# Splitting a weight stream into high and low parts one half chunk further ahead of the matmuls

## The chip, the core and the metric

The kernel runs on one core of a Trainium2 chip. Its engines work side by side, each through its own queue in program order: TensorE (PE in the profile; its weight loads are PEld), VectorE (DVE), ScalarE (ACT), GpSimd (POOL) and SyncE (SP, which only issues DMA transfers here). Engines wait for each other by semaphores. The metric is the device time of one execution in microseconds (us), the median of three runs.

## What is computed

Two layers of a decoder block on 256 tokens of width 1024, all in float32: a half-step SwiGLU feed-forward (ffn1), a mixer that adds dilated attention and a gated linear recurrence, a cross-attention into 256 memory tokens, and a second feed-forward (ffn2).

```python
for l in range(DEPTH):                                   # DEPTH = 2
    x = x + 0.5 * swiglu(rms_norm(x, ffn1_norm[l]), ffn1_w_gu[l], ffn1_w_down[l])
    h = rms_norm(x, mix_norm[l])
    z = h @ w_in[l]                                      # 1024 -> 10752
    ...
    merged = sigmoid(gate_a) * y_a + sigmoid(gate_b) * y_b
    x = x + merged @ w_mix_out[l]
    x = x + cross_attention(rms_norm(x, xattn_norm[l]), rms_norm(mem, mem_norm[l]), ...)
    x = x + 0.5 * swiglu(rms_norm(x, ffn2_norm[l]), ffn2_w_gu[l], ffn2_w_down[l])
return rms_norm(x, final_norm)
```

## The kernel before

**Split weights.** Every product with a weight is made of fp32r matmuls on two parts: `whi`, the weight rounded to fp32r, and `wlo`, the weight minus `whi`. The activations are split in the same way and lie in a `slot` as high and low halves side by side. One weight block is 128x128. In the usual form (`fm`, L325 and L326, and `fm_beside`, L338 and L339) a block takes two matmuls: `whi` against 512 columns (both halves of the activation) and `wlo` against 256 columns.

**The stream.** Class `Stream` holds all weight blocks in the order of their use. A chunk is 16 blocks (1 MB, one DMA, tile `raw`, three buffers); a half chunk is 8 blocks, numbered here from 0 to 535 through the whole program. For each half chunk ACT writes `whi` from `raw` (L104, a cast of 128x1024) and DVE writes `wlo` from `raw` and `whi` (L110). The first four half chunks are made in pieces before the loop (`first`, L74 and L75). The load of chunk c+2 goes into the buffer of chunk c-1, so SP issues it when the last `wlo` of chunk c-1 is done.

**The order.** The program is written out in the order of execution (`manual_schedule`): each engine runs its instructions as the Python code emits them. The clock of that code is `take`, called for each group of blocks. At the first block of half chunk i it runs `on_half`, which is `tick`: the deferred work that has come due (adding a result's halves, L349; multiplying by the norm, L521; activation functions, L522; splitting the result into a `slot`, L279 on ACT and L282 on DVE) and one step of the side work (memory statistics, rope tables, lower bounds, recurrence, attention). Behind that, `prep` emits the casts up to half chunk i+3 and the low parts up to i+2. So what DVE has to do at step i stands in its queue ahead of the low part that PE wants at step i+2. Results are copied out of PSUM by ACT (`L346`) as soon as a `pair` is complete; in the residual form (`Resid.take`) DVE adds them to x (L438), ACT and DVE write the next layer's split operand (L289, L290) and the sum of squares (L376, L378).

**Stages that matter here.** In ffn1 of layer 1 the side work of the whole program (memory statistics, rope tables, lower bounds) runs beside the feed-forward. At the end of the mixer, eight pairs of 12 blocks (`w_att_branch`, `w_hgrn_branch`) are multiplied by the gates (L927, L929) and split; then `mm_resid` of `w_mix_out` runs four outputs side by side (`fm_beside`, 32 blocks), followed by two `fm` of two outputs each (16 blocks each).

**Buffers.** `his` has 5 tiles of 4 KB per partition, `los` 4, and `big`, the pool of the slots, 27.

Of the kernel before, what the change touches and what calls it, by code (L numbers as in the profile page):

```python
# [46 lines left out]
class Stream:  # L47
# [65 lines left out]
    def take(self, descs):  # L113

        n = len(self.order)
        i, o = divmod(n, HALF)
        assert o + len(descs) <= HALF
        self.order.extend(descs)
        if o == 0:
            if i == 0:  # L120
                self.prep(i + 3, i + 2)
            self.on_half()
            self.prep(i + 3, i + 2)
            self.hi.pop(i - 1, None)
            self.lo.pop(i - 1, None)
        s = slice(o * P, (o + len(descs)) * P)
        return self.hi[i][:, s], self.lo[i][:, s]


def build(tc, a, nchunks):  # L130
    nc = tc.nc
    ctx = ExitStack()
    ent = ctx.enter_context
    consts = ent(tc.tile_pool(name="consts", bufs=1))
    raws = ent(tc.tile_pool(name="raws", bufs=3))
    his = ent(tc.tile_pool(name="his", bufs=5))
    los = ent(tc.tile_pool(name="los", bufs=4))
    big = ent(tc.tile_pool(name="big", bufs=27))
    mid = ent(tc.tile_pool(name="mid", bufs=4))
    tmps = ent(tc.tile_pool(name="tmps", bufs=10))  # L140
    tiny = ent(tc.tile_pool(name="tiny", bufs=2))
# [981 lines left out]
```

## Time and profile before

| what | value |
|---|---|
| median of 3 runs | 1645.06 us (1644.39 to 1645.84) |
| profiled execution | 1648.55 us, of which the span from the first to the last instruction is 1646.8 us |
| PE busy | 1624.9 us, 99% of the span |
| PE weight loads busy | 1415.4 us, 86% |
| DVE busy | 1242.6 us, 75% |
| ACT busy | 924.7 us, 56% |
| granted TensorE clock, mean over the span | 0.997 |
| DMA | 288.92 MB, mean 175 GB/s |

The profile is of one execution. The ends of matmuls are modelled and they overlap, so the 99% of PE is not a statement that nothing can be gained; the waits and the distances from start to start tell more. A share of busy time is a mean over stages that differ.

### The profile page before, as it was taken

The page shows a single profiled execution, that of the slowest core. Times are in us where ns is not written, and L with a number is a line of the kernel's source. Part 1 is how long each engine was busy: PE and PEld are TensorE (multiplying, and loading weights), DVE is VectorE, ACT ScalarE, POOL GpSimd, SP SyncE. Part 2 cuts the span into 40 slices and gives each one's busy share as a digit, 9 for nine tenths or more (in the row PEclk, how much of TensorE's full clock was granted, in tenths as well). Part 3 has the DMA queues.
Part 4 walks back from the last instruction along what each step waited for, and adds up shares of the span by engine and source line. Part 5 has one row for each costly group of instructions (what it writes and reads, how often), then busy time and mean ns, then how long its engine had stood idle before and what let it go on. Part 6 is the DMA issues. An engine that isn't in the chain of part 4 may idle for free.

```text
span 1646.8 us, 26215 instructions
## 1 busy us (share of the span) xinstructions
PE 1624.9 (99%) x10818; PEld 1415.4 (86%) x10818; DVE 1242.6 (75%) x1804; ACT 924.7 (56%) x1381; POOL 64.6 (4%) x46
## 2 busy tenths in 40 slices
PE   9999999999999999999999999999999999999998
PEld 7888888888887888888888888888888878888887
DVE  7888577777878777777677776777688787688764
ACT  6666454556555556565455655546565555566642
POOL 0000000102200000000000000001111000000000
PEclk9999999999999999999999999999999999999999
DMA  7555554443445444555445554544344444455552
GB/s 283 185 185 215 183 187 169 155 160 126 176 152 181 179 154 156 199 183 205 179 179 186 198 213 172 193 169 152 132 152 163 169 178 157 152 186 198 181 200 80
DMA packets 41591, 288.92 MB, mean 175 GB/s; under 512 B 4864, under 2 KB 4992, under 8 KB 7424
## 3 DMA queue, kind: packets, MB, share of 16 engines
q1 hardware_dynamic: 41040, 286.67, 48.0%
q8 instruction: 85, 1.39, 0.3%
q10 hardware_dynamic: 432, 0.59, 0.1%
q14 instruction: 34, 0.28, 0.0%
HBM read 286.18 MB, written 1.05 MB: 174 GB/s over the span
## 4 chain that ended last, share of the span: by engine, by line
PE 90%; DVE 5%; ACT 4%; issue 1%; DMA 0%; POOLq 0%; ACTq 0%; DVEq 0%
PE pair L325 48%; PE pair L326 25%; PE pair L299 3%; PE pair L300 3%; PE pair L301 3%; ACT whi L104 2%; PE bank L656 1%; DVE wlo L110 1%; DVE join L349 1%; PE pair L338 1%; DVE join L927 1%; PE pair L754 1%; PE bank L787 1%; ACT join L346 1%; PE pair L339 1%
## 5 line engine op out<-in xcount | busy, mean ns | idle before, releaser
L325 PE MATMUL pair<-slot,whi 128*128 128x512 f32 x3744 | 1321.5, 397 | 0.0
L326 PE MATMUL pair<-slot,wlo 128*128 128x256 f32 x3744 | 1049.1, 280 | 7.2 <-DVE wlo L110 7.2
L325 PEld LDWEIGHTS pair<-slot,whi 128*128 128x128 f32 x3744 | 703.6, 188 | 162.2 <-DVE slot L282 0.4
L326 PEld LDWEIGHTS pair<-slot,wlo 128*128 128x128 f32 x3744 | 707.9, 189 | 10.9 <-DVE wlo L110 9.8
L110 DVE TENSOR_TENSOR wlo<-raw,whi 128x1024 fp32r<-128x1024 f32 x532 | 641.1, 1224 | 27.9 <-ACT whi L104 27.1
L104 ACT CAST whi<-raw 128x1024 fp32r<-128x1024 f32 x532 | 540.0, 1045 | 13.7 <-issue 5.6
L349 DVE TENSOR_TENSOR join<-pair,join 128x512 f32<-128x512 f32 x136 | 93.9, 691 | 122.1 <-ACT join L346 121.8
L346 ACT COPY join<-pair 128x512 f32<-128x512 f32 x136 | 79.3, 584 | 98.4 <-PE pair L326 98.3
L289 ACT ACTIVATE slot<-x,vecs 128x256 fp32r<-128x256 f32 x64 | 30.8, 505 | 138.6 <-DVE x L438 137.2
L522 ACT ACTIVATE tmp<-join 128x256 f32<-128x256 f32 x88 | 36.5, 418 | 117.9 <-DVE join L521 117.8
L279 ACT CAST slot<-join 128x256 fp32r<-128x256 f32 (+1 forms) x120 | 51.8, 435 | 69.3 <-DVE join L929 31.1
L299 PE MATMUL pair<-whi,slot 128*128 128x512 f32 x224 | 88.9, 397 | 0.0
L300 PE MATMUL pair<-wlo,slot 128*128 128x512 f32 x224 | 87.6, 391 | 0.7 <-DVE wlo L110 0.7
L301 PE MATMUL pair<-whi,slot 128*128 128x512 f32 x224 | 87.4, 390 | 0.0
L438 DVE SCALAR_TENSOR_TENSOR x<-pair,x 128x256 f32<-128x256 f32 (+1 forms) x80 | 42.4, 530 | 54.4 <-PE pair L326 49.6
L346 ACT COPY slot<-pair 128x512 f32<-128x512 f32 x48 | 28.1, 585 | 78.9 <-PE pair L326 78.9
L349 DVE TENSOR_TENSOR slot<-pair,slot 128x512 f32<-128x512 f32 x48 | 33.1, 689 | 40.7 <-ACT slot L346 40.7
L521 DVE TENSOR_TENSOR join<-join,bc 128x512 f32<-128x512 f32 x88 | 60.5, 692 | 3.9 <-ACT bc L414 1.2
L890 POOL TENSOR_TENSOR join<-join,sinb 128x512 f32<-128x512 f32 x24 | 43.7, 1820 | 414.1 <-ACT join L889 402.8
L282 DVE TENSOR_TENSOR slot<-join,slot 128x256 fp32r<-128x256 f32 (+1 forms) x120 | 53.4, 454 | 2.8 <-ACT slot L279 2.8
L300 PEld LDWEIGHTS pair<-wlo,slot 128*128 128x128 f32 x224 | 42.1, 188 | 9.6 <-DVE wlo L110 1.6
L290 DVE SCALAR_TENSOR_TENSOR slot<-x,vecs,slot 128x256 fp32r<-128x256 f32 x64 | 29.6, 484 | 27.2 <-ACT slot L289 27.2
(192 smaller groups left out, 1088.7 us busy)
## 6 DMA issues: line engine op xcount, KB each, us to landing
raw<-w SPq DMA_DIRECT2D x266, 1024.0 KB, 4.8
slot<-mem SPq DMA_DIRECT2D x6, 512.0 KB, 6.8
raw<-w SPq DMA_DIRECT2D x3, 512.0 KB, 7.6
y<-slot SPq DMA_DIRECT2D x3, 256.0 KB, 2.3
cst<-cst SPq DMA_DIRECT2D x1, 721.0 KB, 10.2
x<-x SPq DMA_DIRECT2D x2, 256.0 KB, 4.5
x<-x SPq DMA_DIRECT2D x1, 512.0 KB, 7.1
raw<-w ACTq DMA_DIRECT2D x1, 256.0 KB, 5.2
```

The lines of the kernel that those rows point to most:

```text
L104: nc.scalar.copy(self.hi[i], r)
L110: nc.vector.tensor_tensor(self.lo[i], r, self.hi[i].bitcast(F32), op=OP.subtract)
L279: nc.scalar.copy(h, src)
L282: nc.vector.tensor_tensor(l, src, h.bitcast(F32), op=OP.subtract)
L299: nc.tensor.matmul(out, ah, wh, start=first, stop=False)
L300: nc.tensor.matmul(out, ah, wl, start=False, stop=False)
L301: nc.tensor.matmul(out, al, wh, start=False, stop=last)
L325: nc.tensor.matmul(whole[:, i * 512:(i + 1) * 512], wh, act.parts(k), start=k == 0, stop=False)
L326: nc.tensor.matmul(whole[:, i * 512:i * 512 + T], wl, act.hi(k), start=False, stop=k == K - 1)
L346: nc.scalar.copy(d, right)
L349: nc.vector.tensor_tensor(d, left, d, op=OP.add)
L521: nc.vector.tensor_tensor(two(t), two(t), both(n.bc), op=OP.mult)
```

## The change

`take` emits the casts and low parts one half chunk further ahead: up to i+4 and i+3 in place of i+3 and i+2, at the same places of the program. A call of `prep` ahead of the first `tick` falls away; it emitted nothing, since four half chunks are already made by then. To hold the tiles, `his` has 6 tiles in place of 5 and `los` 5 in place of 4; the slots go from 27 to 25, so that the memory used stays the same.

```diff
@@ take @@
         if o == 0:
-            if i == 0:
-                self.prep(i + 3, i + 2)
             self.on_half()
-            self.prep(i + 3, i + 2)
+            self.prep(i + 4, i + 3)
             self.hi.pop(i - 1, None)
             self.lo.pop(i - 1, None)
@@ build @@
-    his = ent(tc.tile_pool(name="his", bufs=5))
-    los = ent(tc.tile_pool(name="los", bufs=4))
-    big = ent(tc.tile_pool(name="big", bufs=27))
+    his = ent(tc.tile_pool(name="his", bufs=6))
+    los = ent(tc.tile_pool(name="los", bufs=5))
+    big = ent(tc.tile_pool(name="big", bufs=25))
```

On each engine the order of everything else stays as it was; the one difference is where the first casts and low parts enter. ACT, at the start of the program, before (L385 are the squares for the first norm, L346 the first copies out of PSUM):

```order
L74 CAST whi_161<-raw_105 128x512
L385 ACTIVATE slot_174<-x_90 128x1024
L385 ACTIVATE slot_175<-x_90 128x1024
L104 CAST whi_198<-raw_123 128x1024
L104 CAST whi_217<-raw_123 128x1024
L104 CAST whi_241<-raw_194 128x1024
L346 COPY join_261<-pair_172 128x512
```

ACT at the same place in the change (lines from L118 on are two lower there):

```order
L74 CAST whi_161<-raw_105 128x512
L383 ACTIVATE slot_174<-x_90 128x1024
L104 CAST whi_181<-raw_123 128x1024
L383 ACTIVATE slot_175<-x_90 128x1024
L104 CAST whi_200<-raw_123 128x1024
L104 CAST whi_223<-raw_177 128x1024
L104 CAST whi_245<-raw_177 128x1024
L344 COPY join_265<-pair_172 128x512
```

Three casts stood ahead of the first copy, now four do; from there on each cast stands where the cast of the half chunk before it stood. The second place is DVE in layer 1 where the side-by-side product of `w_mix_out` ends. Before, `wlo_5110` is half chunk 164, `wlo_5174` is 167, `wlo_5219` is 168 and `wlo_5241` is 169:

```order
L110 TENSOR_TENSOR wlo_5110<-raw_4966,whi_5077 128x1024
L110 TENSOR_TENSOR wlo_5132<-raw_4966,whi_5108 128x1024
L110 TENSOR_TENSOR wlo_5152<-raw_5024,whi_5130 128x1024
L110 TENSOR_TENSOR wlo_5174<-raw_5024,whi_5150 128x1024
L438 SCALAR_TENSOR_TENSOR x_90<-pair_5105,x_90 128x512 x2
L290 SCALAR_TENSOR_TENSOR slot_5194<-x_90,vecs_91,slot_5194 128x256 x2
L378 TENSOR_TENSOR tmp_5104<-tmp_5104,tmp_5200 128x256
L438 SCALAR_TENSOR_TENSOR x_90<-pair_5106,x_90 128x512 x2
L290 SCALAR_TENSOR_TENSOR slot_5205<-x_90,vecs_91,slot_5205 128x256 x2
L378 TENSOR_TENSOR tmp_5104<-tmp_5104,tmp_5210 128x256
L378 TENSOR_TENSOR tmp_5104<-tmp_5104,tmp_5213 128x256
L110 TENSOR_TENSOR wlo_5219<-raw_5075,whi_5172 128x1024
```

DVE at the same place in the change, where `wlo_5116` is half chunk 165, `wlo_5178` is 168 and `wlo_5225` is 169:

```order
L110 TENSOR_TENSOR wlo_5116<-raw_4949,whi_5081 128x1024
L110 TENSOR_TENSOR wlo_5136<-raw_5000,whi_5114 128x1024
L110 TENSOR_TENSOR wlo_5158<-raw_5000,whi_5134 128x1024
L110 TENSOR_TENSOR wlo_5178<-raw_5051,whi_5156 128x1024
L436 SCALAR_TENSOR_TENSOR x_90<-pair_5109,x_90 128x512 x2
L288 SCALAR_TENSOR_TENSOR slot_5198<-x_90,vecs_91,slot_5198 128x256 x2
L376 TENSOR_TENSOR tmp_5108<-tmp_5108,tmp_5204 128x256
L436 SCALAR_TENSOR_TENSOR x_90<-pair_5110,x_90 128x512 x2
L288 SCALAR_TENSOR_TENSOR slot_5209<-x_90,vecs_91,slot_5209 128x256 x2
L376 TENSOR_TENSOR tmp_5108<-tmp_5108,tmp_5214 128x256
L376 TENSOR_TENSOR tmp_5108<-tmp_5108,tmp_5217 128x256
L110 TENSOR_TENSOR wlo_5225<-raw_5051,whi_5176 128x1024
```

The low part of half chunk 168 stood behind the residual work (L438 to L378) and now stands ahead of it; the one behind it is that of 169.

## Rows read from the trace of the kernel before

**Rows 1.** The page: span, then busy time of each engine.

```profile
span 1646.8 us, 26215 instructions
...
PE 1624.9 (99%) x10818; PEld 1415.4 (86%) x10818; DVE 1242.6 (75%) x1804; ACT 924.7 (56%) x1381; POOL 64.6 (4%) x46
```

**Rows 2.** Waits of PE, whole span: who <- whom: us, times, longest.

```profile
PE pair L326 <- DVE wlo L110: 7.2, 8, 1.8
...
PE pair L339 <- DVE wlo L110: 2.2, 2, 1.2
...
PE pair L300 <- DVE wlo L110: 0.7, 2, 0.4
```

**Rows 3.** Waits of PE from 60 to 110 us (ffn1, layer 1).

```profile
PE pair L326 <- DVE wlo L110: 2.8, 4, 1.7
```

**Rows 4.** Waits of PE from 255 to 285 us (mixer, layer 1).

```profile
PE pair L300 <- DVE wlo L110: 0.4, 1, 0.4
```

**Rows 5.** Waits of PE from 470 to 550 us (end of the mixer, layer 1).

```profile
PE pair L326 <- DVE wlo L110: 2.2, 2, 1.8
PE pair L339 <- DVE wlo L110: 1.0, 1, 1.0
```

**Rows 6.** Timeline of PE at one stall: start, us, what, [idle before <- releaser].

```profile
515.42 0.39 PE L338 MATMUL pair<-slot,whi 128*128 128x512 f32 x1
516.81 0.39 PE L339 MATMUL pair<-slot,wlo 128*128 128x256 f32 x1 [1.00 <-DVE wlo L110]
517.03 0.40 PE L338 MATMUL pair<-slot,whi 128*128 128x512 f32 x1
517.27 0.28 PE L339 MATMUL pair<-slot,wlo 128*128 128x256 f32 x1
517.39 0.40 PE L338 MATMUL pair<-slot,whi 128*128 128x512 f32 x1
```

**Rows 7.** Windows: from:to us, then PE, PEld, DVE, ACT, POOL; clock; DMA.

```profile
530.19:533.60 3.41, 3.41 (x12) 2.93 (x13) 2.80 (x5) 1.13 (x4) 0.00 (x0) 0.50 0.40 113
533.60:537.00 3.40, 3.40 (x21) 2.96 (x21) 3.30 (x5) 2.28 (x4) 0.00 (x0) 1.00 0.46 195
```

**Rows 8.** Timeline of DVE in ffn1 of layer 1, with its side work.

```profile
82.25 0.43 DVE L378 TENSOR_TENSOR tmp<-tmp 128x256 f32<-128x256 f32 x1 [0.79 <-ACT tmp L376]
82.60 1.22 DVE L110 TENSOR_TENSOR wlo<-raw,whi 128x1024 fp32r<-128x1024 f32 x1
...
90.12 1.22 DVE L110 TENSOR_TENSOR wlo<-raw,whi 128x1024 fp32r<-128x1024 f32 x1
...
96.19 1.22 DVE L110 TENSOR_TENSOR wlo<-raw,whi 128x1024 fp32r<-128x1024 f32 x1
```

**Rows 9.** Timeline of DVE at the end of the mixer, layer 1.

```profile
515.54 4.62 DVE L110 TENSOR_TENSOR wlo<-raw,whi 128x1024 fp32r<-128x1024 f32 x4
521.75 1.42 DVE L438 SCALAR_TENSOR_TENSOR x<-pair,x 128x512 f32<-128x512 f32 x2 [1.59 <-PE pair L339]
...
528.75 2.35 DVE L110 TENSOR_TENSOR wlo<-raw,whi 128x1024 fp32r<-128x1024 f32 x2
...
534.67 2.35 DVE L110 TENSOR_TENSOR wlo<-raw,whi 128x1024 fp32r<-128x1024 f32 x2
...
540.88 2.35 DVE L110 TENSOR_TENSOR wlo<-raw,whi 128x1024 fp32r<-128x1024 f32 x2
```

**Rows 10.** Timeline of PE, the longest stall of layer 1.

```profile
530.03 0.46 PE L326 MATMUL pair<-slot,wlo 128*128 128x256 f32 x1 [1.85 <-DVE wlo L110]
```

**Rows 11.** Timeline of PE, a transpose in the attention of layer 1.

```profile
431.31 0.27 PE L775 MATMUL pair<-cst,slot 128*128 128x128 f32 x1
```

**Rows 12.** Timeline of ACT, a copy out of PSUM into a slot.

```profile
442.46 0.59 ACT L346 COPY slot<-pair 128x512 f32<-128x512 f32 x1 [1.46 <-PE pair L326]
```

**Rows 13.** Waits of ACT for weight chunks, whole span.

```profile
ACT whi L104 <- DMA raw<-w: 2.4, 2, 1.9
```

**Rows 14.** Line 110: durations in ns (least/median/most) of its queue's waits.

```profile
L110 DVEq EVENT_SEMAPHORE  x110: 21/21/2634, 16.3 to 1626.4; - x110
```

## The prediction

> **What bounds the kernel now.** I read the page first: PE is busy for 1624.9 of 1646.8 us [rows 1], so the time can only come from what PE waits for, or from how fast it runs. On such a figure the Trainium skill ("Perfetto Trace Analysis", Identifying the Most-Contended Engine) says that matmul busy time is a poor measure of headroom, and that the busy share of the weight loads is a better one. That would be 86% here, 231 us of headroom; the rows below bound it far lower, and the sum does without it.
>
> The waits of PE come next. Nearly all of its idle time inside the program ends with a low part that DVE has just written: 7.2 + 2.2 + 0.7 = 10.1 us in 12 stalls [rows 2]. The same view cut into stretches puts them in three places of layer 1: four in ffn1 beside the side work, 2.8 us [rows 3]; one in the mixer, 0.4 us [rows 4]; three at the end of the mixer, 3.2 us [rows 5]. What is left of the total, 0.3 and 3.4 us, belongs to the last two places in layer 2, which runs the same code without the side work.
>
> A stall costs more than its gap. The timeline of one shows it [rows 6]: from L338 to L339 it takes 1.39 us where 0.24 us is normal (517.03 to 517.27), and from there to the next L338 0.22 us where 0.12 us is normal (517.27 to 517.39). That is 1.25 us for a gap of 1.00 us, so about 0.25 us on top. And behind the longest stall, 1.85 us [rows 10], the granted clock falls: for 3.41 us it is 0.50, the 1.2 GHz level, and 12 matmuls run, against 21 in the next 3.40 us at full clock [rows 7]. Nine matmuls of 3.40/21 = 0.16 us are 1.46 us lost. Layer 2 has a stall of the same length [rows 2], and I take 1.4 us for it. All that the low parts cost is then 10.1 + 12 x 0.25 + 2.9 = 16.0 us, and this is the most that the change can give back.
>
> **What the change moves.** No instruction is added or taken away on a computing engine. Step i of the program now ends with the low part of half chunk i+3 in place of i+2. The work that makes DVE late stands ahead of it in either case, so at a given moment DVE has one more half chunk ready. PE spends 8 pairs of matmuls on one, at 0.35 us (517.03 to 517.39 is 0.36 [rows 6]) 2.8 us. A stall by lateness of less than that goes away; one that has built up over a stretch shrinks by 2.8 us in all.
>
> **ffn1, layer 1.** The same place of DVE's round of two half chunks comes at 82.60, 90.12 and 96.19 us [rows 8]: 7.5 and 6.1 us, where PE needs 5.6 us. What DVE waits for in this round is ACT (0.79 us for L376), not PE, so the round will not change when PE comes earlier, and the lateness goes on growing. The four stalls are its sum: 2.8 + 4 x 0.25 = 3.8 us. One half chunk more covers the first 2.8 us, and 1.0 us stays, near 91 and 97 us. Gain 2.8 us.
>
> **Mixer, 270 us.** One stall of 0.4 + 0.25 us behind a block of recurrence work on DVE; a single lateness, and less than 2.8 us. All of it goes, in either layer: gain 1.3 us.
>
> **End of the mixer.** The three stalls of layer 1 have gaps of 0.35, 1.00 and 1.85 us [rows 5, 10]. The first two are one lateness from the gates and go: 0.60 + 1.25 = 1.85 us. For the third, the rows of the order are the argument: half chunk 168 is now made ahead of the residual work, as the last of the four low parts that end at 515.54 + 4.62 = 520.16 us [rows 9]. The question is what is late next. DVE waited 1.59 us for PE before L438; with PE 1.85 us earlier it goes straight on at 520.2 us, so all behind it moves by 1.55 us. Half chunk 169, now first of the pair at 528.75, is ready at 528.75 - 1.55 + 1.2 = 528.4 us. PE would have wanted 168 at 530.03 - 2.0 = 528.0 us, now 1.85 us earlier, 526.2, and 169 at 529.0: 0.6 us to spare. Half chunk 171 is ready at 534.67 - 1.55 + 1.2 = 534.3, wanted at 526.2 + 3 x 2.8 = 534.6. Half chunk 173 is ready by 540.88 - 1.55 + 1.2 = 540.5, wanted at 526.2 + 5 x 2.8 = 540.2. So the long stall and its slow clock go (1.85 + 0.25 + 1.46 = 3.6 us), and in its place come margins of a few tenths of either sign, for which I take off 0.35 us. Gain in layer 1 1.85 + 3.6 - 0.35 = 5.1 us. Layer 2 has gaps of 3.4 us in all: 3.4 + 3 x 0.25 + 1.4 - 0.35 = 5.2 us.
>
> **What it costs.** Three things could, and I set each at nothing. (1) *The slots.* With 25 in place of 27 a new slot takes over memory that was in use more recently. By the buffer addresses of the built program the narrowest case is a slot that ACT writes at 442.46 us [rows 12] and whose memory was last read by the attention's transpose at 431.31 + 0.27 us [rows 11]: 10.9 us, nearly four half chunks. What covers it is that distance; each microsecond that ACT came earlier than that would cost one. (2) *The weight loads.* Load, cast and low part of a chunk all move together by one half chunk, and ACT waited for a chunk only 2.4 us in all [rows 13]. At the start one more cast stands ahead of the first copy out of PSUM, 1 us on ACT, while PE still has two half chunks made in pieces. (3) *Waits.* Counting the rows of the order that name two semaphores, 272 low parts now wait for both the DMA and ACT, before 109. The row for such a wait of DVE's queue shows 21 ns [rows 14]; 163 of them are 3.4 us if nothing hides them. DVE is idle a quarter of the time, so I take 0 and keep 3.4 us as the upper bound. This is the rule that speaks against the change: the Trainium skill ("Perfetto Trace Analysis", Identifying Dependency Chains) says that an instruction waiting on several engines may get EventSemaphore instructions ahead of it. The trace agrees that they are there; what they cost is the row's, not the page's.
>
> **Sum.** 2.8 + 1.3 + 5.1 + 5.2 = 14.4 us. The profiled execution would go from 1648.55 to 1634.2 us, its span from 1646.8 to 1632.4. It lies 3.5 us over the median of the runs, so I predict 1645.06 - 14.4 = 1630.7 us, 0.9% faster. The bounds from the unknown costs are 16.0 us of gain (1629.1) and, with the 3.4 us of waits and another 0.6 us of small stalls, 10.4 us (1634.7).
>
> **Rivals.** *As summed*, 0.72. *The late stall comes back one half chunk on*, 0.14: the margins at 169 to 173 are of tenths, and if DVE's chain is later by 1 us or more than I move it, a stall with slow clock returns, at half chunk 171 or 173, in both layers: 2 x (1.85 + 0.25 + 1.4) = 7 us back, 1637.7 us. For it speaks that DVE's round there, 5.9 to 6.2 us from pair to pair [rows 9], is longer than PE's 5.6; against it that there are only three such rounds. *No change*, 0.06: DVE can't use the lead, because a low part one further ahead waits for something that still comes at the old time, a load above all, with three `raw` buffers as before; 1645 us. Against it is that load, cast and low part move as one. *Slower by the slots*, 0.04: the 10.9 us above are not there, since ACT in the change runs further ahead of the attention's transposes than in this trace. It decides from there on; at 3 us short in each of eight such reuses (four in either layer within 1.7 us of the narrowest) it costs 24 us against the 14 of gain, 1655 us. The last 0.04 I leave to causes that I don't see, on both sides.
>
> A measurement of this kernel tells about 0.2% (3.3 us) from no change. Faster than that: 0.72 + 0.14 and half of the rest, with a part of the no-change case that is really a small gain, 0.90; the same 0.05; slower 0.05. The range reaches from 1628, just under the bound of all stalls gone, to 1637.5, just short of the returned stall; the likeliest case's own is 1629 to 1635.
>
> **What the changed profile would show.** Right: PE's waits for L110 fall from 10.1 to about 1 to 2 us, those left near 91 and 97 us and small ones near 534 to 541 us; no stretch of clock 0.50 between 12 us and the last microseconds; L438 at the end of the mixer no longer waiting for PE; no new releaser of ACT or DVE in the attention. Wrong: a wait of L110's length near 531 to 541 us (second case), PE's waits where they were (third), or ACT's L346 in the attention waiting for PE's transposes (fourth). The prediction is wrong if DVE's round beside the side work, or behind `w_mix_out`, depends on PE in a way that its named waits hide.

## The result, and the profile after

The change makes the kernel faster: 1634.19 us (median of 4 runs, 1632.04 to 1635.23) against 1645.45 us (1644.39 to 1648.01), a ratio of 0.9928 with a 95% interval of 0.9910 to 0.9945. That is 11.3 us less (9.0 to 14.8 by the interval), where 14.4 were forecast; the time lies in the range. The interval alone would not tell 11.3 us from 14.4; what is missing is read from the traces. The profiled execution took 1635.23 us.

The page of the change answers to [rows 1]:

```profile
span 1633.4 us, 26391 instructions
...
PE 1618.6 (99%) x10818; PEld 1414.2 (87%) x10818; DVE 1242.7 (76%) x1804; ACT 924.0 (57%) x1381; POOL 64.6 (4%) x46
```

DVE and ACT do the same work in the same time, and PE's share is 99% as before. The page alone hides what happened. The waits of PE in the change (who <- whom: us, times, longest) answer to [rows 2]; line numbers from L118 on are two lower than before, so that L326 is L324 here, L378 is L376 and L397 is L395:

```profile
PE bank L395 <- DVE tmp L376: 3.2, 2, 1.6
...
PE pair L324 <- DVE wlo L110: 0.6, 2, 0.3
```

The 10.1 us of waiting for low parts in 12 stalls are 0.6 us in two. In their place stands a wait that was not there: the first matmul of the cross-attention's norm (L395) waits for DVE's sum of squares (L376), 1.6 us in either layer. The windows answer to [rows 7] (columns as there). Before, the end of the mixer of layer 2 had the same slow stretch as that of layer 1:

```profile
1342.56:1345.97 3.41, 3.41 (x13) 2.92 (x12) 2.70 (x7) 2.25 (x5) 0.00 (x0) 0.50 0.69 255
```

In the change the same places of both layers run at a clock of 1.00, and so does every window of 10 us between 20 and 1620 us:

```profile
520.00:534.00 14.00, 13.52 (x77) 11.47 (x76) 11.96 (x20) 8.06 (x16) 0.00 (x0) 1.00 0.38 139
1326.00:1339.00 13.00, 13.00 (x75) 11.17 (x74) 10.99 (x18) 7.42 (x14) 0.00 (x0) 1.00 0.37 127
```

The timeline of DVE at the end of the mixer of layer 1 answers to [rows 9]:

```profile
511.58 4.62 DVE L110 TENSOR_TENSOR wlo<-raw,whi 128x1024 fp32r<-128x1024 f32 x4
516.13 1.41 DVE L436 SCALAR_TENSOR_TENSOR x<-pair,x 128x512 f32<-128x512 f32 x2
...
523.13 2.35 DVE L110 TENSOR_TENSOR wlo<-raw,whi 128x1024 fp32r<-128x1024 f32 x2
...
529.05 2.35 DVE L110 TENSOR_TENSOR wlo<-raw,whi 128x1024 fp32r<-128x1024 f32 x2
...
534.11 0.95 DVE L376 TENSOR_TENSOR tmp<-tmp 128x256 f32<-128x256 f32 x2
534.97 2.36 DVE L110 TENSOR_TENSOR wlo<-raw,whi 128x1024 fp32r<-128x1024 f32 x2
```

L436 no longer waits for PE: DVE goes straight on from the four low parts (516.20) and is busy, but for waits on ACT, until the next norm. What is late at the end of that chain is not a low part but the sum of squares, at 534.11 to 535.06. PE shows who wanted it:

```profile
533.24 0.28 PE L324 MATMUL pair<-slot,wlo 128*128 128x256 f32 x1
535.11 0.61 PE L395 MATMUL bank<-cst,tmp 128*128 128x1 f32 x4 [1.59 <-DVE tmp L376]
```

From start to start that is 1.87 us where 0.12 us is normal behind such a matmul [rows 6], so the new stall costs 1.75 us in each layer.

### The profile page after: what moved, and what is told of

The parts are those of the page before. It is cut to its first block, busy times and chain, and to the rows that moved or that the text cites. A ratio compares the mean times of both kernels' runs of the same rounds, so it can differ in the third digit from the quotient of the medians.

```text
span 1633.4 us, 26391 instructions
## 1 busy us (share of the span) xinstructions
PE 1618.6 (99%) x10818; PEld 1414.2 (87%) x10818; DVE 1242.7 (76%) x1804; ACT 924.0 (57%) x1381; POOL 64.6 (4%) x46
## 4 chain that ended last, share of the span: by engine, by line
PE 89%; DVE 5%; ACT 4%; issue 1%; DMA 1%; POOLq 0%; ACTq 0%; DVEq 0%; SPq 0%
PE pair L323 47%; PE pair L324 24%; PE pair L297 3%; PE pair L299 3%; PE pair L298 3%; ACT whi L104 2%; DVE wlo L110 1%; PE bank L654 1%; DVE join L347 1%; DVE join L925 1%; DVE x L436 1%; PE pair L752 1%; PE bank L785 1%; ACT join L344 1%; PE pair L336 1%
## 5 line engine op out<-in xcount | busy, mean ns | idle before, releaser
L324 PE MATMUL pair<-slot,wlo 128*128 128x256 f32 x3744 | 1047.6, 280 | 0.6 <-DVE wlo L110 0.6
L324 PEld LDWEIGHTS pair<-slot,wlo 128*128 128x128 f32 x3744 | 706.9, 189 | 1.9 <-DVE wlo L110 1.2
L110 DVE TENSOR_TENSOR wlo<-raw,whi 128x1024 fp32r<-128x1024 f32 x532 | 641.6, 1225 | 29.2 <-ACT whi L104 28.4
L104 ACT CAST whi<-raw 128x1024 fp32r<-128x1024 f32 x532 | 539.8, 1045 | 13.0 <-PE pair L299 7.4
L520 ACT ACTIVATE tmp<-join 128x256 f32<-128x256 f32 x88 | 36.5, 418 | 117.9 <-DVE join L519 117.9
L277 ACT CAST slot<-join 128x256 fp32r<-128x256 f32 (+1 forms) x120 | 51.8, 435 | 69.4 <-DVE join L927 31.1
L299 PE MATMUL pair<-whi,slot 128*128 128x512 f32 x224 | 87.4, 390 | 0.0
L436 DVE SCALAR_TENSOR_TENSOR x<-pair,x 128x256 f32<-128x256 f32 (+1 forms) x80 | 42.4, 530 | 47.3 <-PE pair L324 45.9
L519 DVE TENSOR_TENSOR join<-join,bc 128x512 f32<-128x512 f32 x88 | 60.5, 692 | 3.9 <-ACT bc L412 1.2
L288 DVE SCALAR_TENSOR_TENSOR slot<-x,vecs,slot 128x256 fp32r<-128x256 f32 x64 | 29.6, 483 | 27.1 <-ACT slot L287 27.1
L299 PEld LDWEIGHTS pair<-whi,slot 128*128 128x128 f32 x224 | 42.0, 188 | 9.0
```

Of the source, the lines that this page charges most:

```text
L104: nc.scalar.copy(self.hi[i], r)
L110: nc.vector.tensor_tensor(self.lo[i], r, self.hi[i].bitcast(F32), op=OP.subtract)
L299: nc.tensor.matmul(out, al, wh, start=False, stop=last)
L324: nc.tensor.matmul(whole[:, i * 512:i * 512 + T], wl, act.hi(k), start=False, stop=k == K - 1)
L436: nc.vector.scalar_tensor_tensor(x, half, self.scale, x, op0=OP.mult, op1=OP.add)
L519: nc.vector.tensor_tensor(two(t), two(t), both(n.bc), op=OP.mult)
```

## The experiments

The theory: the gain is the stalls on low parts and the clock that the longest of them cost, and what is missing against the forecast is the new wait for the sum of squares. Against it stand: the slots cost something, the gain is shared by the whole run, the sums were late all along, or low parts or casts alone would do.

**Fewer slots alone.** The kernel before with one edit:

```diff
-    big = ent(tc.tile_pool(name="big", bufs=27))
+    big = ent(tc.tile_pool(name="big", bufs=25))
```

> The kernel before with 25 slots in place of 27 and nothing else. If the slots cost nothing, as I set them: the time of before, 1645.4 us within 0.2%, and PE's waits for L110 as before, 10.1 us in 12 stalls. If the reuse of slots holds ACT or DVE up (the rival on the other side): up to 24 us slower, with a wait of ACT's L346 or L279 for PE's transposes in the attention.

Measured: ratio 1.0001 (0.9992 to 1.0010), no difference beyond 1.6 us. PE's waits are those of [rows 2] within 0.2 us:

```profile
PE pair L326 <- DVE wlo L110: 7.1, 8, 1.8
...
PE pair L339 <- DVE wlo L110: 2.0, 2, 1.0
...
PE pair L300 <- DVE wlo L110: 0.7, 2, 0.4
```

Fewer slots by themselves cost nothing that the runs can tell. The rival on the other side was about fewer slots together with the lead, and for that the waits of ACT in the change decide:

```profile
ACT whi L104 <- PE pair L299: 7.4, 8, 1.4
...
ACT slot L777 <- PE pair L774: 1.8, 2, 0.9
```

The wait for the attention's transposes (L774) was 1.9 us before and has not grown. The wait of the casts for matmuls of the mixer (L299) has, from 0.9 us; it holds ACT up there, but no wait of PE comes of it.

**Only the low parts ahead.** The change with the casts left where they were:

```diff
-            self.prep(i + 4, i + 3)
+            self.prep(i + 3, i + 3)
...
-    his = ent(tc.tile_pool(name="his", bufs=6))
+    his = ent(tc.tile_pool(name="his", bufs=5))
```

> The low parts one half chunk further ahead (i+3), the casts where they were (i+3), so that DVE takes each low part in the same step as ACT makes its cast; five low tiles, five cast tiles, 25 slots. If the lead of the low parts is all that matters: the time of the change, 1634.2 us. If DVE then stands waiting for the cast of its own step, which ACT makes only behind its own late work: about half of the gain, 1637 to 1643 us, and DVE's wait for L104 rises from 27 us to over 100 us.

Measured: 1828.58 us, ratio 1.1110 (1.1093 to 1.1126), 183 us slower. The second branch had the mechanism, but was far off in size. DVE's waits:

```profile
DVE wlo L110 <- ACT whi L104: 384.4, 293, 4.4
```

and ACT's:

```profile
ACT tmp L520 <- DVE join L519: 193.5, 82, 2.8
...
ACT slot L277 <- DVE join L527: 131.0, 83, 2.6
```

PE's wait for low parts, 10.1 us before, is now the sum of many small ones:

```profile
PE pair L324 <- DVE wlo L110: 58.8, 83, 0.8
```

The two engines wait for each other by turns. The timeline of DVE in ffn1 of this kernel, and then that of ACT, show one round:

```profile
133.92 1.23 DVE L110 TENSOR_TENSOR wlo<-raw,whi 128x1024 fp32r<-128x1024 f32 x1 [1.42 <-ACT whi L104]
...
136.11 0.69 DVE L519 TENSOR_TENSOR join<-join,bc 128x512 f32<-128x512 f32 x1
138.23 1.23 DVE L110 TENSOR_TENSOR wlo<-raw,whi 128x1024 fp32r<-128x1024 f32 x1 [1.42 <-ACT whi L104]
139.37 0.42 DVE L527 TENSOR_TENSOR join<-tmp,join 128x256 f32<-128x256 f32 x1
141.48 1.22 DVE L110 TENSOR_TENSOR wlo<-raw,whi 128x1024 fp32r<-128x1024 f32 x1 [1.69 <-ACT whi L104]
```

```profile
136.84 0.42 ACT L520 ACTIVATE tmp<-join 128x256 f32<-128x256 f32 x1 [2.47 <-DVE join L519]
137.16 1.03 ACT L104 CAST whi<-raw 128x1024 fp32r<-128x1024 f32 x1
139.82 0.41 ACT L277 CAST slot<-join 128x256 fp32r<-128x256 f32 x1 [1.63 <-DVE join L527]
...
140.40 1.05 ACT L104 CAST whi<-raw 128x1024 fp32r<-128x1024 f32 x1
```

L519 on DVE ends at 136.80, L520 on ACT starts at 136.84, the cast behind it at 137.16, and only at its end (138.19) can DVE make the low part; behind that stands L527, for which ACT's L277 waits, and behind L277 stands the next cast. From 133.92 to 141.48 a round of two half chunks takes 7.6 us, against the 5.6 us of PE. In this kernel the cast has to be one half chunk further ahead than the low part, or the two in-order queues become one chain.

**Only the casts ahead.**

```diff
-            self.prep(i + 4, i + 3)
+            self.prep(i + 4, i + 2)
...
-    los = ent(tc.tile_pool(name="los", bufs=5))
+    los = ent(tc.tile_pool(name="los", bufs=4))
```

> The casts one half chunk further ahead (i+4), the low parts where they were before (i+2); six cast tiles, four low tiles, 25 slots. PE waits for low parts, and those stay where DVE's late work puts them: 1645.4 us within 0.2%, with PE's waits for L110 of about 10 us. Rival: the lowness of DVE comes from ACT's casts, and an earlier cast frees it: 1640 us or less, with DVE's wait for L104 (27 us before) near 0.

Measured: ratio 0.9997 (0.9988 to 1.0006), no difference. PE's waits:

```profile
PE pair L324 <- DVE wlo L110: 7.4, 9, 1.8
...
PE pair L337 <- DVE wlo L110: 2.2, 2, 1.2
...
PE pair L298 <- DVE wlo L110: 0.7, 2, 0.4
```

DVE's wait for L104, 27.1 us before, is gone from its list. The sign that the rival named came true and the time did not follow, so the casts were not what made DVE late. It is the low parts' lead that brings the gain, and the casts' lead that makes it possible.

**Layer 2 alone.**

```diff
-            self.prep(i + 4, i + 3)
+            n_ahead = 4 if i >= self.nhalf // 2 else 3
+            self.prep(i + n_ahead, i + n_ahead - 1)
```

> The change from half chunk 268 on (layer 2) alone; the first layer keeps the lead of before, the pools are those of the change. If the stalls of the two layers are independent and their prices are those of the prediction: 0.65 + 5.5 us come back less the new stall of 1.75 us, 4.4 us, 1641.0 us, and PE waits for L110 in layer 1 as before (3.8 + 0.65 + 5.4 us with refill and clock). Rival: a good part of the gain is not from the stalls but from something that the whole run shares (pools, their places in memory): more than 7 us, under 1638.5 us.

Measured: 1642.14 us against 1645.42, ratio 0.9979 (0.9969 to 0.9988): 3.3 us (2.0 to 5.1 by the ratio) of the 11.3. PE's waits (lines are one lower here than in the kernel before):

```profile
PE pair L325 <- DVE wlo L110: 4.9, 6, 1.8
...
PE bank L396 <- DVE tmp L377: 1.6, 1, 1.6
...
PE pair L338 <- DVE wlo L110: 1.0, 1, 1.0
...
PE pair L299 <- DVE wlo L110: 0.4, 1, 0.4
```

The waits of layer 1 are all there, as in [rows 3] to [rows 5], although this kernel has the tiles of the change; those of layer 2 are gone but for the new one. So the gain goes with the stalls, and more tiles without the lead bring nothing. Layer 1 alone was not run; by difference it would have 8.0 us. The expected gain of 4.4 us lies inside the interval, 1.1 us above the median. In the profiled execution a slow stretch that the expectation did not count is the likely reason. Behind the new stall of layer 2,

```profile
1346.98 0.61 PE L396 MATMUL bank<-cst,tmp 128*128 128x1 f32 x4 [1.58 <-DVE tmp L377]
```

the granted clock fell to 0.50, the 1.2 GHz level, for 3.41 us:

```profile
1348.72:1352.13 3.41, 3.41 (x13) 2.82 (x12) 2.60 (x6) 1.69 (x2) 0.70 (x1) 0.50 0.85 293
1352.13:1355.54 3.41, 3.41 (x21) 3.02 (x20) 1.35 (x3) 0.67 (x2) 0.00 (x0) 1.00 0.63 202
```

Eight matmuls fewer at 0.16 us are 1.3 us, and six of the ten runs have this one's mean clock, 0.996. In the profile of the change the same stall had no such stretch behind it.

**The norm's sums one half chunk later.** The change, and in the cross-attention:

```diff
         mn = memn["n"]
+        n.wait = 3
         urgent_norm(n)
```

> The change, with the sums of the cross-attention's norm asked of PE one half chunk later (a wait of 3 steps in place of 2). The new stall of 1.6 us behind w_mix_out in each layer is PE waiting for DVE's last sum of squares; if that is the whole of it, both go, with 0.15 us each on top: 3.5 us less than the change, 1630.7 us. Rival: DVE and ACT are late there in any case, and the stall moves to a low part or to the first copy that waits for the norm: 1633 to 1635 us, with a stall of L324 or a later L412 in its place.

Measured: 1631.11 us (1629.57 to 1631.41), ratio 0.9906 (0.9892 to 0.9920): 3.1 us less than the median of the change. The two intervals overlap, but the slowest of these four runs is faster than the fastest of the change (1632.04). No stall of another kind came up; of PE's waits for DVE this is left:

```profile
PE pair L324 <- DVE wlo L110: 0.6, 2, 0.3
```

and the sums run with no wait in front:

```profile
536.12 0.50 PE L395 MATMUL bank<-cst,tmp 128*128 128x1 f32 x4
```

**The same in the kernel before.** The same line in the kernel with the old lead.

> The kernel before with the later norm alone. In it PE comes to the norm's sums 1.6 us after DVE has them, so nothing waits there and nothing is gained: 1645.4 us within 0.2%. That would show that the wait for the sums is one that the change brought to light. Rival: the sums are late by their place in the program whatever the lead is: 3 us faster.

In the kernel before, the last sum of squares on DVE and the matmul that wants it stand like this; the sum is ready at 540.96, 1.60 us ahead of PE:

```profile
540.01 0.95 DVE L378 TENSOR_TENSOR tmp<-tmp 128x256 f32<-128x256 f32 x2
```

```profile
542.56 0.50 PE L397 MATMUL bank<-cst,tmp 128*128 128x1 f32 x4
```

Measured: ratio 0.9997 (0.9988 to 1.0006), no difference. The sums were not late by themselves; PE came to them later while it stood waiting for a low part a little earlier. With the experiment above this shows that the old stall had covered the new one.

**Two half chunks further, with the later norm.**

```diff
-            self.prep(i + 4, i + 3)
+            self.prep(i + 5, i + 4)
...
-    his = ent(tc.tile_pool(name="his", bufs=6))
-    los = ent(tc.tile_pool(name="los", bufs=5))
-    big = ent(tc.tile_pool(name="big", bufs=25))
+    his = ent(tc.tile_pool(name="his", bufs=7))
+    los = ent(tc.tile_pool(name="los", bufs=6))
+    big = ent(tc.tile_pool(name="big", bufs=23))
```

> The change with the later norm, and two half chunks of lead in place of one (casts to i+5, low parts to i+4, seven and six tiles, 23 slots). What is left of PE's waits for L110 is 0.6 us near 92 and 98 us, 0.9 us with refill; they go: 0.9 us less than the later norm alone, 1630.2 us. By 23 slots a slot is written within 0.2 us of the last read of what lay there before; that read is a transpose whose result the writer copies, so it costs nothing. Rival: the slots now hold ACT or DVE up, and it is slower than the later norm alone by 1 us or more, 1632 us or over, with waits of ACT or DVE for PE in the attention that grew.

Measured: 1630.18 us (1629.79 to 1631.22), ratio 0.9907 (0.9894 to 0.9921), 0.9 us under the median of the kernel with the later norm. That is the expected figure, but the runs don't show the difference: the two kernels were measured at different times, each against its own runs of the kernel before, the two ratios are the same within 0.0001, and the ranges overlap. What the trace shows is that L110 does not occur in the list of PE's waits any more; what is new is small and at the start:

```profile
PE bank L395 <- DVE tmp L389: 0.3, 1, 0.3
```

ACT's wait for chunks has grown from 2.4 us [rows 13], with no wait of PE that comes of it:

```profile
ACT whi L104 <- DMA raw<-w: 4.5, 5, 1.8
```

Both kernels with the lead and the later norm are faster than the change, and faster than the kernel before by 14 to 16 us.

## Why the prediction was right, and where it was off

**The ceiling** of 16.0 us was not passed: with every wait for L110 and both new waits gone, the kernel of two half chunks is 15.7 us under the kernel before (1630.18 against 1645.85; 13.0 to 17.4 by the ratio).

**ffn1** went as worked out. Of four stalls two are left, at 91.90 and 97.98 us, where the text put them:

```profile
91.19 0.39 PE L323 MATMUL pair<-slot,whi 128*128 128x512 f32 x1
91.90 0.39 PE L324 MATMUL pair<-slot,wlo 128*128 128x256 f32 x1 [0.32 <-DVE wlo L110]
```

0.71 us from start to start where 0.24 us is normal are 0.5 us, and 0.4 us at the other (97.34 to 97.98): near the 1.0 us that should stay. DVE's round did not change when PE came earlier; the three low parts that answer to [rows 8] are 7.5 and 6.1 us apart as before:

```profile
83.10 1.22 DVE L110 TENSOR_TENSOR wlo<-raw,whi 128x1024 fp32r<-128x1024 f32 x1
...
90.62 1.22 DVE L110 TENSOR_TENSOR wlo<-raw,whi 128x1024 fp32r<-128x1024 f32 x1
...
96.70 1.22 DVE L110 TENSOR_TENSOR wlo<-raw,whi 128x1024 fp32r<-128x1024 f32 x1
```

**The mixer's stall** at 270 us is gone in both layers.

**The end of the mixer** is where the forecast lost its 3 us. What it said of low parts is borne out: the three stalls are gone with the slow clock, L436 starts behind the low parts without a wait, and the margins at half chunks 169 to 173 were enough. For 173 the change itself can't show this, since its new stall gave DVE 1.75 us more; the kernel with the later norm does. There DVE starts the low part of 173 at 534.91 and has it at 536.13, PE takes its first low part behind the sums at 536.79, and no wait stands there: 0.66 us to spare, where the prediction had it 0.3 us short. The step that failed is "what is late next", priced with 0.35 us per layer. It asked this of low parts alone. The same chain of DVE ends in L378, just ahead of the low part of 173, and PE wants that sum for the norm. By the numbers of the prediction PE is 1.85 + 3.6 = 5.45 us earlier there and DVE 1.55 us; a result that lay 1.6 us ahead of its use before would then be 2.3 us late. In the traces PE without the stall would have come 9.2 us earlier (542.56 to 533.36, which is 0.12 us behind its last matmul) and the sum came 5.9 us earlier (540.96 to 535.06), both counted from the start of the program: 3.3 us less 1.6, 1.7 us late. The term measured 1.75 us in place of 0.35 us in either layer; with it the sum is 14.4 - 2.8 = 11.6 us, and 11.3 were measured, closer than the runs can tell. The later norm gave 3.1 us back, against the 3.5 us of both stalls. This is the sort of case that the second rival stood for (a stall one step on), but at another instruction, and in the profile of the change without its slow clock.

**The clock** was counted with 2.9 us for both layers, as the one profiled execution had it. That term is not the same in every execution, and the length of a stall alone does not decide it: behind 1.58 us in layer 2 of the kernel with the lead there alone the clock fell (above), behind 1.59 us in the change it did not, and at the place of the longest stall of layer 1 in the kernel before with the later norm it stayed at 1.00:

```profile
529.33 0.38 PE L326 MATMUL pair<-slot,wlo 128*128 128x256 f32 x1 [1.71 <-DVE wlo L110]
```

```profile
529.33:540.00 10.67, 10.66 (x59) 9.02 (x60) 9.24 (x16) 5.72 (x11) 0.00 (x0) 1.00 0.54 177
```

So the sum from one profile and the median of other executions need not meet to a microsecond or two.

**The range** held, but in part by luck. The point of 1630.7 us was missed by 3.5 us. The upper part of the range was kept open for a cost of waits on two semaphores and for a low part that is late again; neither came, and it was a third cause, which the prediction did not name, that used the room.

**The costs set at nothing** show nowhere: the slots not in the first experiment, the loads not in PE's waits. The waits for two semaphores came as counted; the line answers to [rows 14]:

```profile
L110 DVEq EVENT_SEMAPHORE  x272: 21/21/2622, 14.7 to 1610.6; - x136
```

The rule of the Trainium skill ("Perfetto Trace Analysis", Identifying Dependency Chains) that they are inserted agrees with the trace, 110 before and 272 after. A cost of them shows nowhere: DVE is busy as long as before, its round in ffn1 is as long, and the sum comes within the interval without one. This was not tried by itself, and up to the 3.4 us of the bound the times alone would not exclude it.

**What stays open.** The profiled spans differ by 13.4 us, the medians by 11.3. The stalls account for the smaller number. Part of the rest is a pace of PE that differs from execution to execution (below): from 145 to 195 us alone the profile of the change has 291 matmuls and that of before 285, which is 1 us. What makes up the remainder was not found; single spans can't be compared to a few microseconds.

## What to carry to other kernels

When a stall of the bounding engine is taken away, list everything that the late engine makes and the bounding engine uses behind the old stall, not only the operand that was waited for: the next result in the same queue is late by the difference of the two shifts less the margin that it had, and its wait is found by the same subtraction. Where one engine's product is another's input in the same step of two in-order queues (cast and low part here), keep a step between them; a lead given to one of the two alone is worth nothing or costs a tenth of the run. A lead of one more buffer pays only for lateness that comes in bursts; against a round that is too long it buys its own length once.

## What the runs showed of the hardware that was not expected

PE ran the same matmuls at two paces without any wait and at the same granted clock. From 145 to 195 us, mostly the down projection of ffn1, the kernel before shows in its windows:

```profile
145.00:195.00 50.00, 50.00 (x285) 43.31 (x284) 34.95 (x53) 26.70 (x41) 0.00 (x0) 1.00 0.57 209
```

The kernel before with the later norm is the same program up to the cross-attention, near 540 us, and shows:

```profile
145.00:195.00 50.00, 50.00 (x291) 44.10 (x289) 35.81 (x55) 27.02 (x41) 0.00 (x0) 1.00 0.58 211
```

285 and 291 matmuls in the same 50 us, 2% apart, in a stage where neither waits; from one pair of matmuls to the next it is 0.353 us in the first and 0.347 us in the second. What sets the pace was not found.

The slow stretch behind a stall comes and goes too. At the end of the mixer the kernel before had it in both layers, the same kernel with the later norm in layer 2 alone, and the one with only the casts ahead in layer 1 alone. Of these six stalls the four of 1.84 or 1.85 us were followed by it and the two of 1.71 and 1.72 us were not, but the stall of 1.58 us above was.

Both may have a share in the spread of the runs of the kernel before, from 1641.64 to 1648.55 us. Of its 41 runs that were taken along with the experiments, the 29 with a mean clock of 0.998 or 0.999 took 1645.3 us in the mean, the 12 with 0.996 or 0.997 took 1646.4 us. That the pace does the rest was not shown, since only one execution of each kernel has a profile.
